# Loading float32 as it is and casting it on GpSimd, in blocks of eight heads, in a batched q·kᵀ kernel

## The chip, the cores and the metric

The kernel runs on one core of one Trainium2 chip. The metric is device time in microseconds (us), as a median of several runs. Runs were taken on several chips, so each kernel is compared only with runs of the kernel before on the same chip.

## The reference

For each of 96 heads (8 batches of 12) the scores of 1024 queries with 1024 keys of 64 numbers:

```python
# q, k: (8, 12, 1024, 64) float32;  out: (8, 12, 1024, 1024) float32
return np.einsum('bhid,bhjd->bhij', q, k).astype(np.float32)
```

The inputs are 50.33 MB and the output 402.65 MB, so nearly all traffic is output. A head's output is 4 MB.

## The kernel before

GpSimd starts the loads. They cast float32 to float16 inside the DMA: each of the 128 partitions reads 8 KB of float32 and 4 KB of float16 is written (for a batch of four heads).

```python
def load(self):                       # class Batch: 1, 1, 2, then 4 heads
    rows = slice(self.first * S, (self.first + self.G) * S)
    self.q_sb = in_pool.tile([P, GMAX * NT, D], F16, tag="q")
    self.k_sb = in_pool.tile([P, GMAX * NT, D], F16, tag="k")
    for src, dst in ((qf, self.q_sb), (kf, self.k_sb)):
        nc.gpsimd.dma_start(
            out=dst[:, : self.R],
            in_=src[rows].rearrange("(p r) d -> p r d", p=P),
        )
```

A head is then transposed on TensorE, because the product needs the 64 numbers of a row on partitions. q goes two row groups at a time (4 transposes); k is transposed twice, once into each half of the partitions (16 transposes), so that both halves of the array find the keys beside their queries. VectorE copies the results out of PSUM, with four copies for q and one for k.

```python
def transpose(self, a):
    ...
    for e in range(4):
        r = a * NT + 2 * e
        nc.tensor.transpose(t_ps[:, e], self.q_sb[:, r : r + 2], ident)
    for t in range(NT):
        rows = self.k_sb[:, a * NT + t]
        nc.tensor.transpose(t_ps[0:64, 4 + t], rows, ident)
        nc.tensor.transpose(t_ps[64:128, 4 + t], rows, ident)
    ...   # DVE: four copies to qT, one to kT
```

The products of a head fill eight PSUM tiles, which ScalarE (ACT, five of them) and VectorE (DVE, three) copy to an output tile; one DMA of 4 MB takes that to HBM. There are four output tiles.

```python
def scores(self, g):
    ...
    for t in range(NT):
        h = (t % 2) * 64
        ps = po_pool.tile([P, S], F32, tag="po")
        for n in range(2):
            nc.tensor.matmul(
                ps[:, n * 512 : (n + 1) * 512],
                qT[h : h + 64, g, t // 2],
                kT[h : h + 64, g, n * 512 : (n + 1) * 512],
            )
        if t in (1, 4, 6):
            nc.vector.tensor_copy(out=o_sb[:, t], in_=ps)
        else:
            nc.scalar.copy(out=o_sb[:, t], in_=ps)
    nc.sync.dma_start(
        out=of[bh].rearrange("(p t) j -> p (t j)", p=P),
        in_=o_sb.rearrange("p t j -> p (t j)"),
    )
```

## Time and profile before

| | before |
|---|---|
| time, median of 3 runs | 1070.88 us (1070.32 to 1071.28) |
| traced span | 1069.6 us |
| DMA engines, mean busy share, 100 to 1000 us | 1.01 |
| busiest compute engine | PE, 59% |
| output packets | 12288 of 32 KB, 1224 ns in the mean |
| large load packets | 5888 (8 KB read, 4 KB written), 322 ns in the median |

The page of the kernel before, from its parts on busy time, slices, queues, the chain that ended last, and instruction groups. In the slices, a digit is the busy share in tenths of one fortieth of the span. A group's line gives busy time, mean ns of one, then the idle time ahead of the group with what ended most of it:

```profile
span 1069.6 us, 8844 instructions
...
PE 627.9 (59%) x3456; PEld 214.0 (20%) x3456; DVE 565.7 (53%) x758; ACT 468.4 (44%) x481; POOL 28.2 (3%) x58
...
DMA  9999999999999999999999999999999999999996
GB/s 213 394 382 386 380 400 414 394 420 396 410 410 384 422 398 410 411 389 419 401 397 424 390 419 401 400 419 389 415 406 399 422 430 430 429 434 432 431 431 292
...
q1 hardware_dynamic: 13824, 402.66, 88.0%
q0 software_dynamic: 7488, 25.17, 11.9%
q8 instruction: 27, 0.44, 0.1%
...
DMA 77%; PE 7%; ACT 7%; DVE 1%; issue 0%; ACTq 0%
...
L114 ACT COPY o_sb<-ps 128x1024 f32<-128x1024 f32 x480 | 467.1, 1014 | 566.5 <-DMA out_dram<-o_sb 359.1
L106 PE MATMUL ps<-kT,qT 64*128 64x512 f16 x1536 | 480.9, 597 | 270.8 <-ACT o_sb L114 227.2
L112 DVE COPY o_sb<-ps 128x1024 f32<-128x1024 f32 x288 | 351.7, 1223 | 374.0 <-DMA out_dram<-o_sb 213.8
...
L92 DVE COPY kT<-t_ps 128x1024 f16<-128x1024 f16 x96 | 118.8, 1237 | 0.0
```

The DMA row is 9 up to the last slice. The chain that ended last is 77% output DMA, and no compute engine is busy for more than 59%. The kernel is bound by its 16 DMA engines. The GB/s row has to be read with care: q0 is counted with 25.17 MB, the float16 that is written, while 50.33 MB are read. A plain load of the same data counts double.

The waits of the kernel before; the columns are total us, number of times and the longest:

```profile
ACT o_sb L114 <- DMA out_dram<-o_sb: 359.1, 87, 7.3
...
DVE o_sb L112 <- DMA out_dram<-o_sb: 213.8, 47, 7.5
```

Both engines that fill output tiles spend hundreds of us waiting for a tile to be sent. That is the slack that hides work done on compute engines.

### The profile page before, as it was taken

The page shows a single profiled execution, that of the slowest core. Times are in us where ns is not written, and L with a number is a line of the kernel's source. Part 1 is how long each engine was busy: PE and PEld are TensorE (multiplying, and loading weights), DVE is VectorE, ACT ScalarE, POOL GpSimd, SP SyncE. Part 2 cuts the span into 40 slices and gives each one's busy share as a digit, 9 for nine tenths or more (in the row PEclk, how much of TensorE's full clock was granted, in tenths as well). Part 3 has the DMA queues.
Part 4 walks back from the last instruction along what each step waited for, and adds up shares of the span by engine and source line. Part 5 has one row for each costly group of instructions (what it writes and reads, how often), then busy time and mean ns, then how long its engine had stood idle before and what let it go on. Part 6 is the DMA issues. An engine that isn't in the chain of part 4 may idle for free.

```text
span 1069.6 us, 8844 instructions
## 1 busy us (share of the span) xinstructions
PE 627.9 (59%) x3456; PEld 214.0 (20%) x3456; DVE 565.7 (53%) x758; ACT 468.4 (44%) x481; POOL 28.2 (3%) x58
## 2 busy tenths in 40 slices
PE   6786455565654656557465564655656567667530
PEld 2222121121211212212122121221211212212100
DVE  5676445464653646547455464554655646655420
ACT  4454344444533445344443444444444445454530
POOL 3000000000000000000000000000000000000000
PEclk8565555555555555555555555555555555555555
DMA  9999999999999999999999999999999999999996
GB/s 213 394 382 386 380 400 414 394 420 396 410 410 384 422 398 410 411 389 419 401 397 424 390 419 401 400 419 389 415 406 399 422 430 430 429 434 432 431 431 292
DMA packets 21353, 428.39 MB, mean 401 GB/s; under 512 B 2368, under 2 KB 2880, under 8 KB 9024
## 3 DMA queue, kind: packets, MB, share of 16 engines
q1 hardware_dynamic: 13824, 402.66, 88.0%
q0 software_dynamic: 7488, 25.17, 11.9%
q8 instruction: 27, 0.44, 0.1%
q14 instruction: 14, 0.11, 0.0%
HBM read 50.33 MB, written 402.65 MB: 424 GB/s over the span
## 4 chain that ended last, share of the span: by engine, by line
DMA 77%; PE 7%; ACT 7%; DVE 1%; issue 0%; ACTq 0%
DMA out_dram<-o_sb 77%; ACT o_sb L114 7%; PE ps L106 6%; DVE kT L92 0%; DVE qT L91 0%; PE t_ps L81 0%; PE t_ps L78 0%; DVE o_sb L112 0%; PE t_ps L82 0%; ACTq L114 0%
## 5 line engine op out<-in xcount | busy, mean ns | idle before, releaser
L114 ACT COPY o_sb<-ps 128x1024 f32<-128x1024 f32 x480 | 467.1, 1014 | 566.5 <-DMA out_dram<-o_sb 359.1
L106 PE MATMUL ps<-kT,qT 64*128 64x512 f16 x1536 | 480.9, 597 | 270.8 <-ACT o_sb L114 227.2
L112 DVE COPY o_sb<-ps 128x1024 f32<-128x1024 f32 x288 | 351.7, 1223 | 374.0 <-DMA out_dram<-o_sb 213.8
L106 PEld LDWEIGHTS <-qT 64*128 64x128 f16 x1536 | 101.0, 109 | 605.2 <-issue 580.0
L91 DVE COPY qT<-t_ps 128x128 f16<-128x128 f16 (+1 forms) x374 | 121.2, 469 | 95.7 <-PE t_ps L82 95.7
L78 PE MATMUL t_ps<-ident,q_sb 128*128 128x128 f16 x384 | 56.4, 299 | 135.9 <-DVE kT L92 130.2
L92 DVE COPY kT<-t_ps 128x1024 f16<-128x1024 f16 x96 | 118.8, 1237 | 0.0
L81 PE MATMUL t_ps<-ident,k_sb 128*64 128x128 f16 x768 | 102.5, 310 | 0.0
L82 PE MATMUL t_ps<-ident,k_sb 128*64 128x128 f16 x768 | 102.4, 310 | 0.0
L81 PEld LDWEIGHTS <-k_sb 128*64 128x64 f16 x768 | 77.5, 165 | 19.8 <-issue 19.4
L82 PEld LDWEIGHTS <-k_sb 128*64 128x64 f16 x768 | 77.4, 164 | 7.5 <-issue 7.5
L78 PEld LDWEIGHTS <-q_sb 128*128 128x128 f16 x384 | 34.6, 127 | 187.2 <-issue 121.3
L64 POOL DMA_DIRECT2D q_sb<-in_q_dram x26 | 14.0, 537 | 767.5 <-PE t_ps L78 766.8
L64 POOL DMA_DIRECT2D k_sb<-in_k_dram x26 | 13.9, 534 | 13.2 <-PE t_ps L82 13.2
L114 ACT ACT_TABLE_LOAD x1 | 1.3, 1283 | 0.7 <-PEq L157 0.7
masks.py:199 POOL TENSOR_SCALAR_AFFINE_SELECT ident<-ident 128x128 f16<-128x128 f16 x1 | 0.4, 362 | 0.0
masks.py:197 POOL MEMSET ident<- 128x128 f16 x1 | 0.3, 271 | 0.0
L157 POOL MEMSET const-float32-0.0<- 128x1 f32 x1 | 0.1, 98 | 0.2 <-issue 0.2
L157 POOL MEMSET const-bfloat16-1.0<- 128x1 bf16 x1 | 0.1, 101 | 0.0
L157 POOL MEMSET const-uint8-127<- 128x1 uint8 x1 | 0.1, 101 | 0.0
L157 POOL MEMSET const-float32-1.0<- 128x1 f32 x1 | 0.1, 98 | 0.0
## 6 DMA issues: line engine op xcount, KB each, us to landing
out_dram<-o_sb SPq DMA_DIRECT2D x96, 4096.0 KB, 36.7
q_sb<-in_q_dram POOLq DMA_DIRECT2D x23, 512.0 KB, 18.1
k_sb<-in_k_dram POOLq DMA_DIRECT2D x23, 512.0 KB, 29.4
q_sb<-in_q_dram POOLq DMA_DIRECT2D x2, 128.0 KB, 3.5
k_sb<-in_k_dram POOLq DMA_DIRECT2D x2, 128.0 KB, 3.6
q_sb<-in_q_dram POOLq DMA_DIRECT2D x1, 256.0 KB, 6.3
k_sb<-in_k_dram POOLq DMA_DIRECT2D x1, 256.0 KB, 7.0
```

The costliest lines, as they stand in the source:

```text
L64: nc.gpsimd.dma_start(out=dst[:, : self.R], in_=src[rows].rearrange("(p r) d -> p r d", p=P),)
L78: nc.tensor.transpose(t_ps[:, e], self.q_sb[:, r : r + 2], ident)
L81: nc.tensor.transpose(t_ps[0:64, 4 + t], rows, ident)
L82: nc.tensor.transpose(t_ps[64:128, 4 + t], rows, ident)
L91: nc.vector.tensor_copy(out=qT[:, g, :, :, a], in_=t_ps[:, 0:4, ms])
L92: nc.vector.tensor_copy(out=kT[:, :, :, a], in_=t_ps[:, 4:12].rearrange("c t (g m) -> c g m t", g=G),)
L106: nc.tensor.matmul(ps[:, n * 512 : (n + 1) * 512], qT[h : h + 64, g, t // 2], kT[h : h + 64, g, n * 512 : (n + 1) * 512],)
L112: nc.vector.tensor_copy(out=o_sb[:, t], in_=ps)
L114: nc.scalar.copy(out=o_sb[:, t], in_=ps)
L157: nc = _bacc.Bacc("TRN2", target_bir_lowering=False, num_devices=1)
```

## The change

The aim was to take work off the transposes and off the DMA. A block is now eight heads in two halves (two, two, four, then eight). The loads are plain float32 on the hardware queues of SP and ACT, and GpSimd casts them into a block buffer where a head of the first half and one of the second lie side by side. One transpose of 128x128 then serves two heads: 8 per head instead of 20. The first half of a block uses partitions 0 to 63, the second 64 to 127. All engines are pinned to written order, with transposes between products. The core of the diff, shortened:

```diff
-        def load(self):
-            ...
-                nc.gpsimd.dma_start(out=dst[:, : self.R], in_=...)      # casts
+        def load(self, n, eng, raw=None):
+            if raw is None:
+                x_sb = in_pool.tile([P, self.elems], F32, tag="x")      # bufs=3
+                raw = x_sb
+            ...
+            pin(eng.dma_start(out=raw, in_=src.rearrange("(p r) d -> p (r d)", p=P)))
+        def cast(self, n):
+            pin(nc.gpsimd.tensor_copy(
+                out=self.halves[n % 2][:, :, n // 2],
+                in_=self.raw[n].rearrange("p (r d) -> p r d", d=D)))
...
-            for e in range(4):
-                nc.tensor.transpose(t_ps[:, e], self.q_sb[:, r : r + 2], ident)
             for t in range(NT):
-                nc.tensor.transpose(t_ps[0:64, 4 + t], rows, ident)
-                nc.tensor.transpose(t_ps[64:128, 4 + t], rows, ident)
+                rows = self.halves[x][:, a * NT + t]      # x: 0 for q, 1 for k
+                pin(nc.tensor.transpose(t_ps[:, t], rows, ident))
...
+            pin(nc.vector.tensor_copy(out=dst, in_=src))   # one eviction for two heads
...
-                h = (t % 2) * 64
+            half, g = divmod(n, self.G)
+            cs = slice(half * D, (half + 1) * D)
...
+    early = out_pool.tile([P, NT, S], F32, tag="out")      # raw data of blocks 0 to 2
+    def refill(i):                                         # blocks[i] and blocks[i+1]
+            for n in range(3): b.cast(n)
+        yield                                              # one head later
+            b.load(3, nc.scalar); b.cast(3)
+            c.load(0, nc.scalar); c.load(1, nc.scalar)
+        ...                                                # two heads later
+            c.load(2, nc.scalar)
```

More of the change, by code (lines that the diff above doesn't have):

```diff
@@ L28 @@
     GMAX = 4
-    assert D == 64 and NT == 8 and BH % GMAX == 0
+    assert D == 64 and NT == 8 and BH % (2 * GMAX) == 0
     qf = q.rearrange("b h s d -> (b h s) d")
@@ L37 @@
     of = out.rearrange("b h i j -> (b h) i j")
-    sizes = [1, 1, 2] + [GMAX] * (BH // GMAX - 1)
-    assert sum(sizes) == BH
+    sizes = [1, 1, 2] + [GMAX] * (BH // (2 * GMAX) - 1)
+    assert 2 * sum(sizes) == BH
     consts = ctx.enter_context(tc.tile_pool(name="consts", bufs=1))
     ident = consts.tile([P, P], F16)
-    in_pool = ctx.enter_context(tc.tile_pool(name="in_pool", bufs=4))
+    in_pool = ctx.enter_context(tc.tile_pool(name="in_pool", bufs=3))
+    half_pool = ctx.enter_context(tc.tile_pool(name="half_pool", bufs=1))
     tr_pool = ctx.enter_context(tc.tile_pool(name="tr_pool", bufs=2))
@@ L48 @@
     pt_pool = ctx.enter_context(
-        tc.tile_pool(name="pt_pool", bufs=1, space=bass.MemoryType.PSUM)
+        tc.tile_pool(name="pt_pool", bufs=2, space=bass.MemoryType.PSUM)
     )
@@ L53, with place @@
     )
-    class Batch:
+    pin = tc.keep_in_program_order
+    class Block:
         def __init__(self, first, G):
             self.first, self.G, self.R = first, G, 8 * G
-        def load(self):
-            rows = slice(self.first * S, (self.first + self.G) * S)
-            self.q_sb = in_pool.tile([P, GMAX * NT, D], F16, tag="q")
-            self.k_sb = in_pool.tile([P, GMAX * NT, D], F16, tag="k")
-            for src, dst in ((qf, self.q_sb), (kf, self.k_sb)):
-                nc.gpsimd.dma_start(
-                    out=dst[:, : self.R],
-                    in_=src[rows].rearrange("(p r) d -> p r d", p=P),
-                )
+            self.elems = self.R * D
+            self.raw = [None] * 4
+        def load(self, n, eng, raw=None):
+            if raw is None:
+                x_sb = in_pool.tile([P, self.elems], F32, tag="x")
+                raw = x_sb
+            self.raw[n] = raw
+            start = (self.first + n // 2 * self.G) * S
+            src = (qf, kf)[n % 2][start : start + self.G * S]
+            pin(eng.dma_start(out=raw, in_=src.rearrange("(p r) d -> p (r d)", p=P)))
+        def place(self, half_sb, at):
+            n = 2 * self.elems
+            self.halves = [
+                half_sb[:, x * half_sb.shape[1] // 2 + at :][:, :n].rearrange(
+                    "p (r h d) -> p r h d", h=2, d=D
+                )
+                for x in range(2)
+            ]
+        def cast(self, n):
+            pin(
+                nc.gpsimd.tensor_copy(
+                    out=self.halves[n % 2][:, :, n // 2],
+                    in_=self.raw[n].rearrange("p (r d) -> p r d", d=D),
+                )
+            )
@@ L69, in alloc, with transpose @@
         def alloc(self):
-            self.qT = tr_pool.tile([P, GMAX * 4 * P], F16, tag="qT")
+            self.qT = tr_pool.tile([P, GMAX * S], F16, tag="qT")
             self.kT = tr_pool.tile([P, GMAX * S], F16, tag="kT")
-        def transpose(self, a):
+        def transpose(self, a, x):
             G, pp = self.G, P // self.G
-            t_ps = pt_pool.tile([P, 12, P], F16, tag="pt")
-            for e in range(4):
-                r = a * NT + 2 * e
-                nc.tensor.transpose(t_ps[:, e], self.q_sb[:, r : r + 2], ident)
+            t_ps = pt_pool.tile([P, NT, P], F16, tag="pt")
@@ L79, in transpose @@
             for t in range(NT):
-                rows = self.k_sb[:, a * NT + t]
-                nc.tensor.transpose(t_ps[0:64, 4 + t], rows, ident)
-                nc.tensor.transpose(t_ps[64:128, 4 + t], rows, ident)
-            qT = self.qT[:, : G * 4 * P].rearrange(
-                "c (g e m a) -> c g e m a", g=G, e=4, m=pp
-            )
-            kT = self.kT[:, : G * S].rearrange(
-                "c (g m a t) -> c g m a t", g=G, m=pp, t=NT
-            )
-            for g in range(G):
-                ms = slice(g * pp, (g + 1) * pp)
-                nc.vector.tensor_copy(out=qT[:, g, :, :, a], in_=t_ps[:, 0:4, ms])
@@ L92, in transpose @@
-            nc.vector.tensor_copy(
-                out=kT[:, :, :, a],
-                in_=t_ps[:, 4:12].rearrange("c t (g m) -> c g m t", g=G),
-            )
-        def scores(self, g):
-            bh = self.first + g
-            qT = self.qT.rearrange("c (g e m) -> c g e m", e=4, m=P)
+                rows = self.halves[x][:, a * NT + t]
+                pin(nc.tensor.transpose(t_ps[:, t], rows, ident))
+            if x == 0:
+                dst = self.qT[:, : G * S].rearrange(
+                    "c (g t m a) -> c g t m a", g=G, t=NT, a=G
+                )[:, :, :, :, a]
+                src = t_ps.rearrange("c t (g m) -> c g t m", g=G)
+            else:
+                dst = self.kT[:, : G * S].rearrange(
+                    "c (g m a t) -> c g m a t", g=G, a=G, t=NT
+                )[:, :, :, a]
+                src = t_ps.rearrange("c t (g m) -> c g m t", g=G)
@@ L100, in scores @@
+            pin(nc.vector.tensor_copy(out=dst, in_=src))
+        def scores(self, n, side):
+            half, g = divmod(n, self.G)
+            cs = slice(half * D, (half + 1) * D)
+            qT = self.qT.rearrange("c (g t m) -> c g t m", t=NT, m=P)
             kT = self.kT.rearrange("c (g j) -> c g j", j=S)
@@ L102, in scores @@
             for t in range(NT):
-                h = (t % 2) * 64
                 ps = po_pool.tile([P, S], F32, tag="po")
-                for n in range(2):
-                    nc.tensor.matmul(
-                        ps[:, n * 512 : (n + 1) * 512],
-                        qT[h : h + 64, g, t // 2],
-                        kT[h : h + 64, g, n * 512 : (n + 1) * 512],
-                    )
+                for j in range(2):
+                    js = slice(j * 512, (j + 1) * 512)
+                    pin(nc.tensor.matmul(ps[:, js], qT[cs, g, t], kT[cs, g, js]))
@@ L111, in scores @@
                 if t in (1, 4, 6):
-                    nc.vector.tensor_copy(out=o_sb[:, t], in_=ps)
+                    pin(nc.vector.tensor_copy(out=o_sb[:, t], in_=ps))
                 else:
-                    nc.scalar.copy(out=o_sb[:, t], in_=ps)
-            nc.sync.dma_start(
-                out=of[bh].rearrange("(p t) j -> p (t j)", p=P),
-                in_=o_sb.rearrange("p t j -> p (t j)"),
+                    pin(nc.scalar.copy(out=o_sb[:, t], in_=ps))
+                if t in side:
+                    side[t]()
@@ L118, in scores @@
+            pin(
+                nc.sync.dma_start(
+                    out=of[self.first + n].rearrange("(p t) j -> p (t j)", p=P),
+                    in_=o_sb.rearrange("p t j -> p (t j)"),
+                )
             )
-    batches, first = [], 0
+    blocks, first = [], 0
     for G in sizes:
-        batches.append(Batch(first, G))
-        first += G
-    AHEAD = 3
-    for b in batches[:AHEAD]:
-        b.load()
-    make_identity(nc, ident)
-    batches[0].alloc()
-    for a in range(batches[0].G):
-        batches[0].transpose(a)
@@ L132 @@
-    for i, b in enumerate(batches):
-        if i + AHEAD < len(batches):
-            batches[i + AHEAD].load()
-        nxt = batches[i + 1] if i + 1 < len(batches) else None
+        blocks.append(Block(first, G))
+        first += 2 * G
+    early = out_pool.tile([P, NT, S], F32, tag="out")
+    raw = early.rearrange("p t j -> p (t j)")
+    half_elems = 2 * GMAX * NT * D
+    half_sb = half_pool.tile([P, 2 * half_elems], F16, tag="half")
+    at = 0
+    for b in blocks[:3]:
+        for n in range(4):
+            piece = raw[:, 2 * at + n * b.elems :][:, : b.elems]
+            b.load(n, (nc.sync, nc.scalar)[n % 2], piece)
+        b.place(half_sb, at)
+        at += 2 * b.elems
@@ new lines @@
+    for n in range(3):
+        blocks[3].load(n, (nc.sync, nc.scalar)[n % 2])
+    make_identity(nc, ident)
+    for b in blocks[:3]:
+        for n in range(4):
+            b.cast(n)
+    def refill(i):
+        b = blocks[i] if i < len(blocks) else None
+        c = blocks[i + 1] if i + 1 < len(blocks) else None
+        if b:
+            half_sb = half_pool.tile([P, 2 * half_elems], F16, tag="half")
+            b.place(half_sb, 0)
+            for n in range(3):
+                b.cast(n)
+        yield
+        if b:
+            b.load(3, nc.scalar)
+            b.cast(3)
+        if c:
+            c.load(0, nc.scalar)
+            c.load(1, nc.scalar)
+        yield
+        yield
+        if c:
+            c.load(2, nc.scalar)
@@ L136 @@
+    blocks[0].alloc()
+    for x in range(2):
+        blocks[0].transpose(0, x)
+    todo = []
+    for i, b in enumerate(blocks):
+        nxt = blocks[i + 1] if i + 1 < len(blocks) else None
         if nxt:
             nxt.alloc()
-        for g in range(b.G):
-            b.scores(g)
-            if nxt:
-                for a in range(g * nxt.G // b.G, (g + 1) * nxt.G // b.G):
-                    nxt.transpose(a)
+        for n in range(2 * b.G):
+            side = {}
+            if nxt and n < nxt.G:
+                side = {
+                    1: lambda: nxt.transpose(n, 0),
+                    6: lambda: nxt.transpose(n, 1),
+                }
+            b.scores(n, side)
+            for job in todo:
+                next(job, None)
+            if nxt and n == nxt.G - 1 and i > 0:
+                todo.append(refill(i + 2))
+                next(todo[-1])
+                if n == 2 * b.G - 1:
+                    next(todo[-1])
```

## The prediction

> **What bounds it now.** The 16 DMA engines, end to end. The page's slices show them at 9 tenths in 39 of 40; the queue table gives 88.0% of 16 engines' span to outputs and 11.9% to loads. The chain that ended last is 77% "DMA out_dram<-o_sb". PE (59%), DVE (53%) and ACT (44%) have slack: ACT waits 359.1 us and DVE 213.8 us for output buffers (the waits). Four heads take 44.4 us with loads (steps of the chain, 83 to 838 us), 39.6 us without (from 917 us). The trace's packets add up to the span: 12288 output packets of 32 KB at 1224 ns are 940 us of 16 engines; load packets are 126.5 us, of which 5888 big ones (8 KB read as float32, 4 KB written as float16) at 322 ns are 118.9.
>
> **What the change does.**
> - Outputs: unchanged, 940 us.
> - Loads: the DMA no longer casts. HBM reads stay 50.33 MB; writes into SBUF double (counted bytes 428 to about 453 MB). That should not double their cost, for reading already sets the pace: plain 8 KB packets in the same trace (the runtime's own queue) take a median 309 ns. Estimate: 5632 packets of 8 KB at 309 ns, 108.8 us; 512 of 4 KB at 160 ns, 5.1; 1024 of 2 KB at 85 ns, 5.4: 119 against 126.5, a saving of 7 us, on the bound itself.
> - Transposes: 20 per head become 8 (PE about 261 to 110 us); DVE evictions, four of 469 ns and one of 1237 per head, become one of about 1.24 us (240 to 119 us). All off the chain, worth 0: waits for output buffers grow instead.
> - New: 60 casts on GpSimd, the big ones of 2048 elements per partition. The trace has no such cast. The Trainium skill, "GPSIMD Engine Reference", section "Engine selection", calls one-input work there roughly line rate; my estimate from it is 2 to 4 us each, on an idle engine; no run shows it yet. At four per block of eight heads (88 us) they harm nothing below about 8 us each.
> - Waits in written order: ACT's loads wait for casts, but are issued a head (10 us) or more after them; their semaphore lanes point only at DMAs long done. PE's transposes need the fourth load, issued three heads ahead. Up to three outputs (30 us) are queued, so such a stall should not empty the queue.
> - Start: first output at about 18 us (17.0 before), but 7.3 MB of loads (17 us) fill the DMA until then. Tail: only a few engines worked from 1061 to 1067 us; if that belongs to the software queue, up to 5 us more are gained.
>
> The Trainium skill, "DMA: Bandwidth & Descriptors", section "Issuing engines are not separate DMA queues", says all queues share the same 16 engines; so moving loads to SP and ACT adds no bandwidth. This trace agrees: with two queues mixed the share stays 1.00 to 1.01.
>
> **Predicted: 1062 us**, 8 in 10 between 1050 and 1073. Faster by over 2%: 0.06; within 2%: 0.90; slower by over 2%: 0.04.
>
> **What would show it.** DMA at 9 throughout; 8 KB load packets at about 309 ns; output packets near 1220 ns; DVE near 470 us busy, PE near 490; longer output waits on ACT and DVE; casts of 2 to 4 us, ACT hardly waiting on GpSimd.
>
> **What would make it wrong.** Casts of 8 us or more, stalling ACT and PE until the output queue empties; doubled SBUF writes slowing 8 KB packets or the outputs beside them; a gap at the start, where one output buffer serves the early loads; or hardware queues alone keeping the engines fuller than 428 GB/s.

## The result, and the profile after

The kernel after takes 1070.81 us (median of 4 runs, 1069.99 to 1070.87); the kernel before took 1070.82 us in the same rounds (4 runs). The ratio is 0.9998, with a 95% interval of 0.9981 to 1.0016. A ratio here is the mean time of one kernel's fast runs over that of the other's of the same rounds, so it is not quite the ratio of the medians quoted. The time has not changed; 1062 us was forecast.

The page of the kernel after, the same parts as before:

```profile
span 1069.1 us, 6245 instructions
...
PE 752.0 (70%) x2304; PEld 270.0 (25%) x2304; DVE 506.9 (47%) x384; ACT 476.3 (45%) x481; POOL 91.6 (9%) x62
...
DMA  9999999999999999999999999999999999999996
GB/s 391 419 407 426 433 429 433 427 429 433 429 432 430 432 432 424 437 428 432 429 429 425 431 432 430 421 436 431 424 425 434 429 432 431 432 432 433 431 431 265
...
q1 hardware_dynamic: 14976, 406.85, 88.8%
q10 hardware_dynamic: 6912, 46.14, 10.4%
q8 instruction: 18, 0.29, 0.1%
...
DMA 76%; PE 15%; ACT 4%; POOL 1%; DVE 1%; issue 0%; ACTq 0%; SPq 0%; POOLq 0%
...
L128 PE MATMUL ps<-kT,qT 64*128 64x512 f16 x1536 | 666.5, 618 | 253.3 <-ACT o_sb L132 226.9
L132 ACT COPY o_sb<-ps 128x1024 f32<-128x1024 f32 x480 | 475.0, 1013 | 551.5 <-DMA out_dram<-o_sb 310.7
L130 DVE COPY o_sb<-ps 128x1024 f32<-128x1024 f32 x288 | 353.1, 1227 | 498.4 <-DMA out_dram<-o_sb 364.7
...
L88 POOL CAST half_sb<-x_sb 128x2048 f16<-128x2048 f32 x44 | 82.2, 1893 | 766.7 <-PE t_ps L103 547.7
...
L115 DVE COPY qT<-t_ps 128x1024 f16<-128x1024 f16 x48 | 110.6, 2304 | 13.7 <-PE t_ps L103 13.7
...
L115 DVE COPY kT<-t_ps 128x1024 f16<-128x1024 f16 x48 | 58.3, 1215 | 16.0 <-PE t_ps L103 16.0
```

The DMA row is still 9 from end to end. The GB/s row rose from about 400 to about 430, which is the counting effect just described. Read side, both kernels move the same 452.98 MB, and between 100 and 1000 us they move 428.8 GB/s before and 429.7 after (worked out from the packet records of the traces). The Trainium skill, "HBM Reference", section "Specifications (TRN2)", says that a core streaming alone measures about 425 GB/s, bounded by its 16 DMA engines; this agrees. So does "DMA: Bandwidth & Descriptors", section "Issuing engines are not separate DMA queues": moving the loads from GpSimd to SP and ACT has brought no bandwidth.

The waits of the kernel after:

```profile
DVE o_sb L130 <- DMA out_dram<-o_sb: 364.7, 83, 7.1
ACT o_sb L132 <- DMA out_dram<-o_sb: 310.7, 82, 6.5
...
ACT o_sb L132 <- POOL half_sb L88: 11.4, 2, 7.2
```

The two output waits together rose from 572.9 to 675.4 us. Compute work did disappear, and it turned into waiting for the DMA.

### Three things the packet records tell

The trace records each DMA packet's start, duration, size and queue, though not its engine. I rebuilt 16 engines by following packets that start where another ends. Between 100 and 900 us this gives, beside the recorded duration, the time from one start to the next on an engine:

```
packet                               median duration   start to start: mean, median
before: 8 KB read, 4 KB written            322 ns          305 ns   304 ns
after:  8 KB plain                         309 ns          308 ns   306 ns
before: 32 KB output                      1213 ns         1221 ns  1214 ns
after:  32 KB output                      1213 ns         1218 ns  1210 ns
```

A casting packet is recorded as 322 ns, but the next packet of its engine is recorded as starting about 18 ns before it ends. It holds its engine for 305 ns, no longer than a plain one. One can see that the durations overlap without rebuilding anything. All durations before, over 16 engines, sum to 1070.4 us, but the engines had only the time from about 2.5 us (the first loads) to 1062.0 us (the mean of the last landings, below), which is 1059.5 us. After, the sum is 1061.8 us and the time from about 1.7 to 1059.7 us is 1058.0 us. The sum of durations fell by 8.6 us; the time that the engines needed fell by 1.5, or by about 3 if one leaves out the 1.8 us that the kernel after lost to a stall, shown next.

The second is when bytes moved. How far the kernel after is ahead, in bytes read or written at 433 GB/s:

```
at us          5    10    30    60    70   100   160   400   800  1000
ahead, us   +1.1  +2.1  +2.0  +1.5  +0.3  +0.5  +1.1  +2.1  +2.1  +2.4
```

It gains 2 us at the start: its DMA begins 0.8 us earlier, and the rest builds up by 10 us, while the small packets of the first loads run (why was not tested). It loses nearly all of it by 70 us, and drifts ahead again by 2 us in the next 900. The windows show the start and the loss; columns are window, its length, busy us (and instructions) of PE, PEld, DVE, ACT and POOL, the granted TensorE clock, the DMA share and GB/s. Before:

```profile
2.00:4.00 2.00, 0.00 (x0) 0.00 (x0) 0.00 (x0) 0.02 (x1) 2.00 (x5) 1.00 0.75 97
...
52.00:56.00 4.00, 4.00 (x26) 1.26 (x26) 1.86 (x2) 2.25 (x3) 0.00 (x0) 0.50 1.06 409
56.00:60.00 4.00, 3.62 (x10) 0.50 (x7) 3.96 (x7) 2.93 (x4) 0.00 (x0) 0.50 0.91 334
```

After:

```profile
2.00:4.00 2.00, 0.00 (x0) 0.00 (x0) 0.00 (x0) 0.00 (x0) 0.00 (x0) 1.00 1.00 351
...
52.00:56.00 4.00, 0.00 (x0) 0.00 (x0) 0.00 (x0) 0.00 (x0) 0.00 (x0) 0.50 0.77 330
56.00:60.00 4.00, 0.00 (x0) 0.00 (x0) 0.00 (x0) 0.00 (x0) 1.86 (x1) 0.50 1.07 459
```

At 2 to 4 us the DMA share is 1.00 against 0.75. From 52 to 60 us no PE instruction starts. The chain of the kernel after tells what it waited for (start, us, what):

```profile
41.53 16.56 DMA x_sb<-in_k_dram
```

This is the fourth load of the first big block, which could start only after a cast had freed a buffer.

The third is the end. An output DMA lands once on each of the 16 engines, and the kernel ends with the last engine of the last output. Means of the last output's landings, and how much later the last engine is ("lag"):

```
                 mean landing    last engine later by    traced span
before             1062.0 us           6.7 us             1069.6 us
after              1059.7 us           8.1 us             1069.1 us
```

The mean engine of the kernel after is done 2.3 us earlier, and the last engine gives 1.4 of it back. Thus three questions for experiments: is a casting load really no dearer, does compute hold the start back, and what makes the last engine late?

### The profile page after: what moved, and what is told of

Same layout as the page of the kernel before. It is cut to its first block, busy times and chain, and to the rows that moved or that the text cites. A ratio compares the mean times of both kernels' runs of the same rounds, so it can differ in the third digit from the quotient of the medians.

```text
span 1069.1 us, 6245 instructions
## 1 busy us (share of the span) xinstructions
PE 752.0 (70%) x2304; PEld 270.0 (25%) x2304; DVE 506.9 (47%) x384; ACT 476.3 (45%) x481; POOL 91.6 (9%) x62
## 4 chain that ended last, share of the span: by engine, by line
DMA 76%; PE 15%; ACT 4%; POOL 1%; DVE 1%; issue 0%; ACTq 0%; SPq 0%; POOLq 0%
DMA out_dram<-o_sb 70%; PE ps L128 12%; ACT o_sb L132 4%; DMA x_sb<-in_k_dram 3%; DMA x_sb<-in_q_dram 2%; PE t_ps L103 2%; POOL half_sb L88 1%; DVE o_sb L130 0%; DMA early<-in_q_dram 0%; DVE qT L115 0%; DVE kT L115 0%; ACTq L132 0%; SPq L75 0%; POOLq L88 0%; SPq L136 0%
## 5 line engine op out<-in xcount | busy, mean ns | idle before, releaser
L128 PE MATMUL ps<-kT,qT 64*128 64x512 f16 x1536 | 666.5, 618 | 253.3 <-ACT o_sb L132 226.9
L132 ACT COPY o_sb<-ps 128x1024 f32<-128x1024 f32 x480 | 475.0, 1013 | 551.5 <-DMA out_dram<-o_sb 310.7
L128 PEld LDWEIGHTS <-qT 64*128 64x128 f16 x1536 | 196.9, 135 | 657.2 <-issue 649.8
L88 POOL CAST half_sb<-x_sb 128x2048 f16<-128x2048 f32 x44 | 82.2, 1893 | 766.7 <-PE t_ps L103 547.7
L103 PE MATMUL t_ps<-ident,half_sb 128*128 128x128 f16 x768 | 97.8, 307 | 29.3 <-POOL half_sb L88 29.3
L115 DVE COPY qT<-t_ps 128x1024 f16<-128x1024 f16 x48 | 110.6, 2304 | 13.7 <-PE t_ps L103 13.7
L103 PEld LDWEIGHTS <-half_sb 128*128 128x128 f16 x768 | 73.1, 140 | 106.5 <-issue 73.6
L115 DVE COPY kT<-t_ps 128x1024 f16<-128x1024 f16 x48 | 58.3, 1215 | 16.0 <-PE t_ps L103 16.0
L88 POOL CAST half_sb<-early 128x512 f16<-128x512 f32 (+1 forms) x12 | 8.7, 755 | 5.6 <-DMA early<-in_q_dram 5.3
## 6 DMA issues: line engine op xcount, KB each, us to landing
x_sb<-in_q_dram SPq DMA_DIRECT2D x2, 1024.0 KB, 11.5
```

Of the source, the lines that this page charges most:

```text
L88: nc.gpsimd.tensor_copy(out=self.halves[n % 2][:, :, n // 2], in_=self.raw[n].rearrange("p (r d) -> p r d", d=D),)
L103: pin(nc.tensor.transpose(t_ps[:, t], rows, ident))
L115: pin(nc.vector.tensor_copy(out=dst, in_=src))
L128: pin(nc.tensor.matmul(ps[:, js], qT[cs, g, t], kT[cs, g, js]))
L132: pin(nc.scalar.copy(out=o_sb[:, t], in_=ps))
```

## The experiments

The theories at the outset were these. A: what a load costs its engine is set by the bytes read, so casting and plain loads cost the same and no gain was there to lose; compute lies off the bound. B: the recorded durations are what counts, so plain loads save 5 to 7 us, which something gives back. C: the waits of the written order, on casts and evictions, give a gain back. Fifteen runs followed, three of them repeats without a new edit. All gave the right result.

### Every load twice, casting or plain (b_extra_cast, b_extra_plain)

The kernel before, with each load repeated into a tile that nobody reads; the tile's type is the only difference of the two.

```diff
+            j_q = junk_pool.tile([P, GMAX * NT, D], F16, tag="j_q")   # F32 in b_extra_plain
+            j_k = junk_pool.tile([P, GMAX * NT, D], F16, tag="j_k")
-            for src, dst in ((qf, self.q_sb), (kf, self.k_sb)):
+            for src, dst in ((qf, self.q_sb), (kf, self.k_sb), (qf, j_q), (kf, j_k)):
```

> Before with every load issued a second time, casting to float16 in the DMA, into a tile nobody reads: 50.33 MB more read. Theory A (a DMA engine is occupied by a load packet for its start-to-start time, 305 ns for the cast packet of 8 KB read, and the 17 ns more in its recorded duration overlap the next packet): 6,000 packets' worth at 305 ns over 16 engines plus the small ones, +117 to +121 us, about 1190 us. Theory B (the recorded duration, 322 ns, is what a packet costs the engine): +126 us, about 1197 us.

> The same, with the second load going to a float32 tile, so without the cast, from the same queue. Theory A: the plain packet occupies an engine for 306 to 308 ns, so the same +117 to +122 us; the two kernels agree within 2 us, this one if anything slower. Theory B: durations of 309 against 322 ns make this one 5 to 7 us faster than the kernel with the extra cast loads.

Measured: 1208.26 us with casting extra loads (ratio 1.1273, 1.1253 to 1.1293) and 1207.55 with plain ones (1.1271, 1.1254 to 1.1288). The pair is equal, which speaks against B. The sizes, 136 us, are larger than expected. Nothing paced the extra loads, so they ran ahead on the queue of the real ones. The waits of b_extra_cast show that:

```profile
PE t_ps L83 <- DMA q_sb<-in_q_dram: 161.5, 6, 42.2
```

In the kernel before, this wait is not among the ten largest. The comparison is thus blurred by a wait common to both, and was repeated with paced loads.

### Extra loads, paced (b_paced_cast, b_paced_plain)

From the eighth head on, each batch's extra loads are read by one small copy a batch later, so that they cannot run ahead.

```diff
+            self.extra = self.first >= 8
+            if self.extra:
+                self.j_q = junk_pool.tile([P, GMAX * NT, D], F16, tag="j_q")   # or F32
+                self.j_k = ...
+                for src, dst in ((qf, self.j_q), (kf, self.j_k)):
+                    nc.gpsimd.dma_start(out=dst[:, : self.R], in_=...)
...
+            if self.extra and a < 2:
+                junk = (self.j_q, self.j_k)[a]
+                nc.vector.tensor_copy(out=self.kT[:, 8 * a : 8 * a + 8], in_=junk[:, 0, 0:8])
```

> Before with the loads of the last 22 batches issued a second time (46.1 MB, 5632 packets), casting, into a tile that VectorE touches once per batch, so that the extra loads cannot run ahead and crowd out the real ones as in the first pair. Theory A (occupancy 305 ns a packet): +107 to +110 us, about 1179 us. Theory B (duration 322 ns): +113 us or more, about 1185 us.

> The same with the extra loads in float32, not cast. Theory A: 306 to 308 ns a packet, +107 to +111 us; within 2 us of the kernel with the paced cast loads. Theory B: 4 to 6 us faster than it.

Measured: 1187.54 us casting (6 runs, 1176.7 to 1190.93; ratio 1.1066, 1.1026 to 1.1107) and 1197.08 plain (6 runs, 1188.27 to 1207.19, one of them slow and left out of the ratio; ratio 1.1168, 1.1129 to 1.1207). Plain loads on the software queue are slower, by 9.5 us in the medians of all runs and by 10.9 us in the means of the fast ones. That is the opposite of B, and also outside what A allowed. From the packet records, start to start: 305.8 ns for casting packets and 310.9 for plain ones, and 1238.6 and 1240.5 ns for the outputs beside them. The mean of the last landings is 1179.5 against 1185.6 us, and the last engine is 6.0 against 15.7 us later. So a plain packet is no cheaper than a casting one, and plain loads on this queue also leave the engines less even. This settles the question of B; why the lag grows does not follow from it.

### Plain loads and GpSimd casts alone (b_plain_loads)

The kernel before, with its loads in float32 on the same GpSimd queue, cast by GpSimd. The transposes, the evictions and the order stay.

```diff
+    raw_pool = ctx.enter_context(tc.tile_pool(name="raw_pool", bufs=2))
-            for src, dst in ((qf, self.q_sb), (kf, self.k_sb)):
+            for src, dst in ((qf, self.q_raw), (kf, self.k_raw)):
+        def cast(self): ...
+            for dst, src in ((self.q_sb, self.q_raw), (self.k_sb, self.k_raw)):
+                nc.gpsimd.tensor_copy(out=dst[:, : self.R], in_=src[:, : self.R])
-    AHEAD = 3
+    AHEAD = 2
```

> One part of the change alone: before, with float32 loads from the same queue and the casts on GpSimd; transposes, matmuls, scheduling and the software queue stay. Theory A: 1069 to 1073 us, same as before, and load packets again 305 to 308 ns apart. Theory B: 5 to 7 us faster, 1063 to 1066 us, because nothing else of the change is there to give the gain back. The unevenness at the end (last engine 6.7 us after the mean of the 16 in before, 8.1 us in after) stays at 4 us or more under A; if B and a loss in the rest of the change were true, it need not.

Measured: 1081.05 us, ratio 1.0093 (1.0078 to 1.0109). It is slower. Windows of b_plain_loads:

```profile
6.00:8.00 2.00, 0.92 (x16) 0.78 (x15) 1.03 (x2) 0.00 (x0) 1.14 (x2) 1.00 0.03 12
8.00:10.00 2.00, 1.43 (x6) 0.42 (x5) 0.86 (x2) 0.38 (x1) 1.64 (x4) 1.00 0.34 74
...
14.00:16.00 2.00, 1.96 (x16) 0.74 (x17) 1.89 (x2) 1.49 (x2) 0.73 (x3) 1.00 0.66 225
```

Loading only two batches ahead, it leaves the DMA nearly idle at 6 to 10 us; 3.7 us are lost at the start. The mean landing is 1066.7 us, 4.7 later than before; the last engine is 11.5 us later than the mean instead of 6.7, which is another 4.8. The steady rate is that of the kernel before. Again there is no gain from plain packets.

### The evictions and casts twice (a_work_twice, a_casts_twice)

Two runs of the kernel after, with the casts and the evictions of transposes each done twice, and later with the casts alone twice.

```diff
+            for _ in range(2):
                 pin(nc.gpsimd.tensor_copy(...))            # both runs
...
-            pin(nc.vector.tensor_copy(out=dst, in_=src))
+            for _ in range(2):                             # a_work_twice alone
+                pin(nc.vector.tensor_copy(out=dst, in_=src))
```

> After, with each eviction of a transpose done twice on VectorE (+169 us busy there, to about 676) and each cast twice on GpSimd (+91 us busy). Theory A: compute is off the bound, time within 2 us of after, 1069 to 1073 us, and the waits for output buffers shrink by about as much as was added. Rival C (the written order of the engines with its early stalls is what took back the 7 us forecast): longer casts and evictions lengthen those stalls, so 3 us or more slower.

Measured for a_work_twice: 1084.27 us, ratio 1.012 (1.0103 to 1.0137). Windows of a_work_twice:

```profile
20.00:24.00 4.00, 3.76 (x18) 1.57 (x18) 3.88 (x4) 2.17 (x3) 2.31 (x3) 1.00 0.26 113
64.00:76.00 12.00, 5.30 (x24) 2.53 (x25) 6.17 (x7) 1.93 (x2) 3.79 (x2) 1.00 0.69 289
120.00:140.00 20.00, 13.52 (x54) 5.76 (x54) 15.48 (x13) 6.89 (x7) 3.79 (x2) 1.00 0.80 323
```

The DMA share drops to 0.26, 0.69 and 0.80 there. By bytes moved, it is 12.3 us behind the kernel before at 160 us and only 9.9 at 1000 us. So A, "compute off the bound", holds only after 160 us. In the first 160 us C is right: longer casts and evictions reach the DMA there, as the three windows show. That few outputs are queued yet is my explanation and was not measured.

> After, with each cast on GpSimd done twice and the evictions once. The run with both doubled lost its 13 us before 160 us of the span. If the casts held the start back there (the output buffer that serves as load buffer comes free only after the twelve early casts), this run loses 3 us or more, with the DMA row low around 20 to 24 us; if the evictions on VectorE did, it stays within 2 us of after (1069 to 1073 us).

Measured for a_casts_twice: 1077.98 us, ratio 1.0057 (1.004 to 1.0074). The mean landing is 1066.0 us against 1059.7 for the kernel after, and by bytes it is 5.3 us behind the kernel before at 160 us, where the kernel after is 1.1 ahead. So about 6.4 of the 13.4 us that a_work_twice lost against the kernel after by then are the casts', the rest the evictions'. After that it loses nothing more.

This shows that casts and evictions set the pace at the start. It does not measure what the kernel after lost to them without doubling. That is bounded by its own trace, 1.8 us between 10 and 70 us. A version with a fourth raw buffer, which would have taken the stall away, did not build: a buffer of 128 KB had 127.59 KB left. So this stays at the size read from the trace.

### More instruction fetches, through GpSimd (a_more_fetches)

The traces have one more difference: queue q8 carries instruction fetches, 27 packets before and 18 after. They are 16 KB each, take about 930 ns on one of the same 16 engines, and come to 64 bytes for each TensorE row (6914 rows before, 4610 after, at 256 a packet). The Trainium skill, "Runtime: NRT & Kernel Launch", section "Instruction fetch mechanics", has the mechanism: each engine's instruction memory is refilled in 16 KiB blocks of 256 instructions by a DMA queue of its sequencer, at a cost it calls "mostly hidden". One engine that gets more such packets than others could be the late one. The first attempt added instructions to GpSimd, which is mostly idle in the kernel after:

```diff
+            if b.first + n >= 16:
+                for _ in range(84):
+                    pin(nc.gpsimd.memset(tiny, 0.0))
```

> After, with 84 tiny memsets on GpSimd after each head from the 17th on: 6720 instructions more, which the instruction queue must fetch in packets of 16 KB (18 before, about 44 now, some 24 us of DMA engine time more), with no more data and no more work on the bound. Theory D (the unevenness of the engines at the end comes from instruction fetches, which fall on single engines and never get evened out): the last engine's lag behind the mean of the 16 grows from 8 us by 3 us or more, and the time with it. If the unevenness has another source, time and lag stay within 2 us of after's.

Measured: 1299.36 us, ratio 1.2134. The group of added instructions in a_more_fetches:

```profile
L208 POOL MEMSET tiny<- 128x1 f16 x6720 | 681.7, 101 | 383.8
```

The run says nothing of fetches. GpSimd became the bound: its 681.7 us of memsets and the gaps between them held back the casts and through them everything (its chain is 59% GpSimd). Besides, its fetches ran on q14 in 8 KB packets, of which there were 66 instead of 14; q8 stayed at 18.

### The kernel after again (after_again)

A repeat without edit, to have its trace twice.

> The changed kernel once more, for a second trace and a closer ratio to before on this chip: same as before within 0.3%, the mean of the engines' last landings about 2 us ahead of before's trace and the last engine's lag behind that mean 7 to 9 us. A lag that differs by several us from run to run would mean that the end is decided by chance, not by the kernel.

Measured: 1071.42 us, ratio 1.0005 (0.9993 to 1.0017), mean landing 1059.5 us, lag 8.6. So both the unchanged time and the earlier mean with the later last engine are reproducible.

### More TensorE rows (a_more_pe, b_more_pe)

Products of one element, which cost TensorE 160 ns each and are overwritten by the real product: 22 per head from the 17th on, 1760 products and as many weight loads. The same edit in both kernels.

```diff
+                if t == 0 and self.first + n >= 16:
+                    for _ in range(22):
+                        one = qT[cs, g, t, 0:1]
+                        pin(nc.tensor.matmul(ps[0:1, 0:1], one, kT[cs, g, 0:1]))
```

> After, with 22 one-element matmuls ahead of each head's first product from the 17th head on, their result overwritten: 3520 rows more in TensorE's program (4610 to 8130). The instruction queue q8 moved exactly 64 bytes for each TensorE row (27 packets of 16 KB for 6914 rows, 18 for 4610), so it should move about 32 packets now, some 13 us more of DMA engine time. Theory D (the fetches make single engines lag): the last engine's lag behind the mean of the 16 (8.1 and 8.6 us in the two traces of after) grows by 2 us or more and the time by about as much, 1073 us or more. If the lag has another source: time within 1.5 us of after's, the lag 7 to 9 us. TensorE's busy time may rise by 100 to 200 us, off the bound in both cases.

Measured for a_more_pe: 1079.31 us, ratio 1.007 (1.0057 to 1.0082), which is 0.65%, or about 7 us, above the ratio of after_again. Page of a_more_pe, span, busy time and the fetch queue:

```profile
span 1076.5 us, 9765 instructions
...
PE 824.5 (77%) x4064; PEld 310.3 (29%) x4064; DVE 507.5 (47%) x384; ACT 477.3 (44%) x481; POOL 91.7 (9%) x62
...
q8 instruction: 31, 0.51, 0.2%
```

PE is busy for 77% and the DMA row is 9 throughout, so TensorE did not become the bound. The mean landing is 1060.8 us, 1.1 to 1.3 later than without, and the lag is 14.5 us instead of 8.1 and 8.6. Most of the loss is one late engine.

> Before with the same 3520 extra rows in TensorE's program (6914 to 10434, so 41 fetch packets of 16 KB for 27), from the 17th head on. If each fetch costs the last engine as much as in the same test on the changed kernel (13 more fetches, 8 us), the time rises by 5 us or more, to 1076 us or above, and the lag of the last engine from 6.7 to 11 us or more. If it stays within 2 us of before, the kernel with casting loads takes fetches better than the one with plain loads, which would explain its smaller lag at 27 fetches.

Measured for b_more_pe: 1076.36 us, ratio 1.0053 (1.0039 to 1.0067), with 41 packets on q8. The mean landing is 1062.9 (0.9 later), the lag 10.2 instead of 6.7. That is 0.53%, or 5.7 us. In both kernels 13 or 14 more fetches went with 6 to 7 us more, about 0.4 to 0.5 us each, where even shares would make it 930 ns / 16 = 0.06 us. The fetches would explain this only if nearly all of them fell on the late engine, and the traces don't name engines.

The landings can test it. Each output lands once on each of the 16 engines, so the lag can be followed from output to output. The last load is through by 870 us in these kernels, so from about 895 us on no load disturbs the picture. Over 13 outputs:

```
              lag at the start and end of the stretch    growth per output
before           5.0 us at  897,   6.7 us at 1023              0.13 us
after            7.0 us at  894,   8.2 us at 1021              0.09 us
b_more_pe        7.3 us at  897,  10.2 us at 1024              0.22 us
a_more_pe       12.2 us at  895,  14.5 us at 1022              0.18 us
```

The last engine falls back a little at nearly every output. That ends between 1011 and 1033 us, shortly before TensorE's last instruction (1034 to 1041 us). A fetch looks different: where one can be told apart, an engine falls back by 1 to 2 us at once, and it is another engine. In the kernel after, the fetch at 937 us moves the second-last engine from 4.1 to 6.1 us behind the mean, while the last one stays at 7.5; in b_more_pe, the fetch at 1034 us moves the second-last one from 5.3 to 6.9, while the last one stays at 10.2. At no output of this stretch does the last engine lose more than 0.4 us. So here the fetches don't make the last engine late.

Single output packets are longer while the added products run. From 890 us on there are 15 bursts of 22 products in each kernel. At 12 of them in a_more_pe and 14 in b_more_pe an output packet of 1325 to 1350 ns is in flight, where the median is 1213; outside the bursts there is none. The kernels before and after have one such packet each in that stretch. The growth is 0.09 us per output more than without the products, in both kernels. If it was the same over the 80 heads that have them, that is 7 us (an estimate from these figures), and the times rose by 7 and 5.7 us. So in this stretch the loss goes with executing the added rows, not with fetching them. How they reach the packets of one engine, no run here shows, so the cause of the late engine stays open.

### The kernel before again, for its trace (before_again)

> The kernel before once more, for a second trace: time 1070 to 1072 us; the mean of the engines' last landings near 1062 us and the lag of the last engine behind it near 6.7 us, if these belong to the kernel; several us off, if they are chance.

Measured: 1071.59 us (one run, state unknown). Mean landing 1061.6 us and lag 7.3, beside 1062.0 and 6.7 in the first trace. The lag of one kernel thus varies by about 0.6 us from trace to trace, and the difference of before and after, 6.7 and 7.3 against 8.1 and 8.6, is small but the same in both pairs.

### Fewer TensorE rows in the kernel before (b_fewer_pe)

This run was made while the fetches were still the suspect: if they make the last engine late, fewer rows should help the kernel before. GpSimd writes k twice side by side, and one transpose then serves both halves: 12 transposes per head instead of 20.

```diff
+            self.k2_sb = tr_pool.tile([P, GMAX * NT, 2 * D], F16, tag="k2")
+            for x in range(2):
+                nc.gpsimd.tensor_copy(out=self.k2_sb[:, : self.R, x * D : (x + 1) * D],
+                                      in_=self.k_sb[:, : self.R])
...
-                nc.tensor.transpose(t_ps[0:64, 4 + t], rows, ident)
-                nc.tensor.transpose(t_ps[64:128, 4 + t], rows, ident)
+                rows = self.k2_sb[:, a * NT + t]
+                nc.tensor.transpose(t_ps[:, 4 + t], rows, ident)
```

> Before with one transpose of k per tile for two (GpSimd writes k twice side by side, one transpose then fills both halves of the partitions): TensorE's program falls from 6914 to 5378 rows, 21 fetch packets for 27, with the loads still casting. Theory D, with 0.4 us a fetch (5.5 us for 14 more in the test on before, 7.9 us for 13 on after): 2 to 3 us faster than before, ratio 0.997 to 0.998, the last engine's lag about 4 to 5 us. If fetches mattered only when added: same as before.

Measured: 1069.12 us, ratio 0.9982 (0.9968 to 0.9996), the best of all kernels run, if only by 0.2%. Page of b_fewer_pe:

```profile
span 1066.3 us, 7382 instructions
...
q8 instruction: 21, 0.34, 0.1%
```

The lag is 6.5 us, no shorter than before, where 4 to 5 were expected. The gain came in the mean landing, 1058.9 us, 3 us earlier. Six packets fewer are worth 6 x 930 ns / 16 = 0.35 us of it. So the fetch theory does not explain the gain either.

The packet records tell where the 3 us are, though not why: an output packet took 1220.3 ns in the mean (recorded, 100 to 900 us) against 1224.6 before, and an engine has 768 of them, which makes 3.3 us. The same step divides all DMA-bound traces without paced loads: 1223.8 to 1225.3 ns in the seven with 20 transposes per head, 1219.9 to 1221.8 in the seven with 12 or 8, the kernel after among them. The added one-element products made no such step (1225.3 and 1221.1).

### Fewer rows with a hardware-queue start (b_fewer_hw)

The attempt to join the best of both: b_fewer_pe, with the first three batches loaded as float32 through SP and ACT and cast by GpSimd, for the 2 us that the kernel after gained at the start.

```diff
+                if early is not None:
+                    at = 2 * self.first * NT + n * self.R
+                    raw = early[:, at : at + self.R]
+                    (nc.sync, nc.scalar)[n].dma_start(out=raw, in_=...)
+                    nc.gpsimd.tensor_copy(out=dst[:, : self.R], in_=raw)
+                    continue
```

> The same with the first three batches loaded in float32 from SP and ACT and cast on GpSimd, as the change does at the start; all later loads cast in the DMA. If the changed kernel's 2 us at the start can be had apart from its larger lag at the end: 1 to 2 us faster than the kernel with fewer rows, some 4 us faster than before, ratio 0.995 to 0.997. If the casts hold back the later loads, which GpSimd issues behind them, it is no faster or slower than that kernel.

Measured: 1072.85 us, ratio 1.0017 (1.0005 to 1.003). The timeline of GpSimd in b_fewer_hw (start, us, engine, line, operation):

```profile
8.48 1.04 POOL L70 CAST q_sb<-early 128x1024 f16<-128x1024 f32 x1 [2.03 <-DMA early<-in_q_dram]
9.46 1.04 POOL L70 CAST k_sb<-early 128x1024 f16<-128x1024 f32 x1
...
11.56 0.67 POOL L72 DMA_DIRECT2D q_sb<-in_q_dram  x1
```

GpSimd issues the fourth batch's loads at 11.56 us, because it stood behind six casts that wait for data and two of the copies of k; the kernel before issues them from 4.63 us. About 5 us of the start are lost. The lag is 5.8 us. The combination as written isn't better; its start could be mended by issuing that load first, which I did not run.

### The plain loads again (b_plain_again)

> The kernel with plain loads and GpSimd casts but the old transposes (27 fetch packets) for a second trace: the lag of its last engine was 11.5 us, against 6.7 and 7.3 us in the two traces of before. If plain loads widen the lag, it is again 9 us or more; near 7 us if the first was chance.

Measured: 1080.68 us (one run, state unknown), mean landing 1067.1 us, lag 10.9. The lags of this kernel are thus 11.5 and 10.9 us, where the kernel before has 6.7 and 7.3 with as many fetches. The longer lag is reproducible. That the plain packets are its cause is not shown: this kernel also casts on GpSimd and loads only two batches ahead, and the table below has plain loads without it.

### The ends of all the kernels side by side

One trace each, taken on several chips; a_more_fetches is left out, for its end is not the DMA's.

```
                 loads                        fetches (q8)   mean landing   lag
before           casting, GpSimd queue             27          1062.0       6.7
before_again     casting, GpSimd queue             27          1061.6       7.3
b_more_pe        casting, GpSimd queue             41          1062.9      10.2
b_fewer_pe       casting, GpSimd queue             21          1058.9       6.5
b_plain_loads    plain, GpSimd queue               27          1066.7      11.5
b_plain_again    plain, GpSimd queue               27          1067.1      10.9
b_fewer_hw       casting but the first three       21          1064.1       5.8
b_extra_cast     casting, all twice                27          1198.9       6.6
b_extra_plain    casting, and plain once more      27          1197.5       6.4
b_paced_cast     casting, nearly all twice         27          1179.5       6.0
b_paced_plain    casting, and plain once more      27          1185.6      15.7
after            plain, SP and ACT queues          18          1059.7       8.1
after_again      plain, SP and ACT queues          18          1059.5       8.6
a_casts_twice    plain, SP and ACT queues          18          1066.0       8.9
a_work_twice     plain, SP and ACT queues          18          1071.9       9.0
a_more_pe        plain, SP and ACT queues          31          1060.8      14.5
```

No single rule orders these rows. The lag rose where TensorE rows were added. With 27 fetches, three rows with plain loads have lags of 10.9 to 15.7 us, but b_extra_plain has 6.4, as short as its casting partner. The kernel after has a lag 1.3 to 1.4 us longer than before, and neither its plain loads nor its fetches are shown to be the reason.

## Why the prediction was right or wrong

The prediction had the bound right and missed the size: 1062 us was forecast, and 1070.81 measured, inside its range of 1050 to 1073 but with no gain at all.

- **The failed step** is "119 against 126.5, a saving of 7 us, on the bound itself". It took the recorded duration of a packet for the time that it holds its engine. Its 309 ns for plain packets came true, but the 322 ns of a casting packet overlap the next packet by 18 ns; start to start it is 305 ns against 308. For 352 large packets on an engine the change is worth 352 x 3 ns, 1 us, to the bad, not 13 ns each to the good; the drift of 2 us ahead over 900 us fits the outputs' 3 ns in size (768 of them on an engine, 2.3 us, less that 1 us). Both pairs of extra loads confirm it: plain was equal in one, and about 10 us dearer in the other. The same paragraph carried the warning: "The trace's packets add up to the span." Engines that start at 2.5 us and on average end 7 us early can't be filled by durations that add up to the whole span, unless durations overlap.
- **"All off the chain, worth 0"**, said of the transposes, is in doubt. In b_fewer_pe, where only transposes were taken away and GpSimd copies put in their place, the output packets got 4 ns shorter and the kernel about 2 us faster; the kernel after has the same shorter packets. Why is not shown.
- **"Tail: ... if that belongs to the software queue, up to 5 us more are gained"**: it does not belong to it. With hardware queues alone, the lag of the last engine was 8.1 and 8.6 us, against 6.7 and 7.3 with the software queue.
- **"Such a stall should not empty the queue"** holds after 160 us, and not before. The fourth load's stall at 52 to 60 us cost the lead of the start nearly in full, and doubled casts and evictions lost 12 us by 160 us and nothing later.
- **The start**: "first output at about 18 us" was 19.6 us by its issue, 17.0 before. Yet its first packet ran at 20.4 us against 20.7, since the loads ahead of it were through sooner. The feared gap at the start did not come: the DMA share is 1.00 or more from 2 to 14 us.
- **Outputs unchanged**: nearly, 1221 ns against 1224 in the mean, which is the 2 us of drift. **Casts of 2 to 4 us**: 1.89 us, just under. The Trainium skill, "GPSIMD Engine Reference", section "Engine selection", calls one-input work roughly line rate, and 2048 elements in 1893 ns are 1.08 per ns. ACT waited for GpSimd only twice, 11.4 us in all.
- **DVE near 470 us**: 506.9. The term that was off is the eviction of q, put at 1.24 us like that of k; it takes 2.30 us. **PE near 490 us**: 752.0. The count of transposes was right; the products' busy time rose from 480.9 to 666.5 us at nearly the same duration (597 and 618 ns), so they overlap less. I put that to the row halves: before, consecutive products alternate between partitions 0 to 63 and 64 to 127; after, all of a head use one half. No run tests this. Both misses are off the bound and cost nothing.
- **"Longer output waits on ACT and DVE"**: in sum yes (572.9 to 675.4 us), for ACT alone no (359.1 to 310.7).

Where the expected gain went, then: most of it never existed. What was real is 2 us at the start, lost by 70 us; 2 us over the steady stretch; and 1.4 us of that given back by a later last engine. What makes the last engine late, and why fewer transposes go with shorter output packets, stays open.

## What to carry to other kernels

Before pricing a DMA change from recorded packet durations, check that they are occupancy: compare them with the time from one packet's start to the next on an engine, or their sum with the time the engines really had. In a DMA-bound kernel, compute work that the steady state hides still counts while the pipeline fills, so read the first stretch on its own. And where all engines are full, look at how late the last one is against the mean; a gain in the mean can be lost there. A suspect for the delay has to be seen on the late engine itself: following the lag from output to output cleared the fetches here, where a count of them had fitted.

## What the Trainium skill lacked or had wrong

- "DMA: Bandwidth & Descriptors" doesn't say what a casting load costs. Here it is its bytes read: 305 ns start to start for 8 KB read and 4 KB written, against 308 ns for 8 KB plain.
- "Perfetto Trace Analysis", section "DMA Engine Tracks", says that slices show actual busy time. In this trace the record of a casting packet is 322 ns and overlaps the next by 18 ns, so the sum of records, 1070.4 us, is more than the 1059.5 us that the engines had.
- "Runtime: NRT & Kernel Launch", section "Instruction fetch mechanics", has the 16 KiB blocks of 256 instructions, and this agrees (27 packets for 6914 TensorE rows). It calls the cost "mostly hidden", and does not say that the blocks take time on the engines that move data: a packet is about 930 ns here, and a single engine falls back by 1 to 2 us at one. What they cost the kernel is not separated: the 6 to 7 us that went with 13 or 14 blocks more aren't shown to be theirs, for where the engines could be followed, it was not the last one that a fetch held.
- "DMA: Bandwidth & Descriptors", section "Latency and other measured facts", has as its best guess that slow engines come from the rings of the software queue and calls that specific to it. Here the last engine, whose number the trace does not give, lagged 8.1 and 8.6 us with hardware queues alone, and 6.7 and 7.3 with a software queue. In both kernels it went on falling back, by about 0.1 us per output, when no loads were left.
- "SBUF — State Buffer", section "Door 1", lets 2-byte elements be strided up to 8 for free. The eviction of q writes fp16 in steps of four elements and takes 2.30 us, that of k writes runs of eight and takes 1.22 us, for the same 128x1024; their reads from PSUM differ as well, and no run here separates the two.
